# Transposing the FFN's gated values by VectorE blocks and a way through DRAM instead of by TensorE

## The chip, the cores and the metric

The kernel runs on one core of one Trainium2 chip. The core has five engines that work side by side, each through its own list of instructions in order: TensorE (PE, matrix products; PEld is its load of weights), VectorE (DVE), ScalarE (ACT), GpSimd (POOL) and SyncE (SP), which here issues the DMA transfers of the weights. The metric is the device time of one execution in microseconds (us), the median of several.

## The reference

Two layers of a decoder trunk for 256 tokens of width 1024, all in float32. In each layer stand two SwiGLU FFNs, one before and one after the token mixers and the cross attention:

```
D_FF = ((8 * D_MODEL // 3 + 127) // 128) * 128        # 2816

def swiglu(x, w_gate, w_up, w_down):
    return (jax.nn.silu(x @ w_gate) * (x @ w_up)) @ w_down

for l in range(DEPTH):                                # 2
    h = h + 0.5 * swiglu(rms_norm(h, ffn1_norm[l]), ffn1_w_gate[l], ffn1_w_up[l], ffn1_w_down[l])
    ...
    h = h + 0.5 * swiglu(rms_norm(h, ffn2_norm[l]), ffn2_w_gate[l], ffn2_w_up[l], ffn2_w_down[l])
return rms_norm(h, final_norm)
```

So four FFNs are computed. The change touches only what lies between the product of gate and up and the product with `w_down`: that product needs the gated values with the 2816 hidden columns on the partitions, and the gate and up products leave them with the tokens there.

## The kernel before

Every operand of a large product is split into a high and a low part (float32r), and a product is three matmuls: high by high, low by high, high by low. The weights come in **chunks** of 2048 columns by 128 partitions (1 MB). `fetch` loads a chunk into `wr` on SyncE's queue (3 buffers), ScalarE copies it to `wh` in two halves, and VectorE writes the rest to `wl`, also in halves (3 buffers each).

`linear` goes over the chunks and, within a chunk, over the two blocks of 128 tokens. For one chunk and one block it issues 12 matmuls of 128x512 into a PSUM bank `lin`; this is a **half tile**, and `begin` and `tick` around it count the clock `now` by which the other chains of work go on. After the last chunk it calls `evac` for each block.

`ffn` computes the 2816 hidden columns in 11 **groups** of 256. One group is two chunks: 512 columns, 256 of gate and 256 of up, for 1024 input rows. Groups 0 and 1 share a pass, so chunks 0 to 3 belong to both; group g from 2 on uses chunks 2g and 2g+1. Then two passes of six chunks each multiply by `w_down`. `evac` makes `sg` (silu of gate, ScalarE) and `toks` (`sg` times up, VectorE) per token block, and after the second block starts the chain `hidden`. Two half tiles later `hidden` lets PE transpose the four 128x128 blocks into a PSUM bank `ht`, and ScalarE and VectorE split that into `hid`, which the down passes read.

PE works in the order in which the program is written. The order of the other engines' instructions is made by a scheduler when the program is built. Each engine then keeps to its order and waits by semaphores where an operand or a buffer is not there yet.

Of the kernel before, what the change touches and what calls it, by code (L numbers as in the profile page):

```python
# [11 lines left out]
F32 = mybir.dt.float32  # L12
# [7 lines left out]
P = 128  # L20
# [3 lines left out]
NB = S // P  # L24
KD = D // P
DFF = 2816
KF = DFF // P
# [125 lines left out]
def program(tc, a, out, upto="all"):  # L153
    nc = tc.nc
    act, dve, pool, pe = nc.scalar, nc.vector, nc.gpsimd, nc.tensor
    ctx = ExitStack()

    def sb(name, bufs):
        return ctx.enter_context(tc.tile_pool(name=name, bufs=bufs))
# [6 lines left out]
    fp = sb("fp", 2)  # L166
    sp = sb("sp", 4)
    mp = sb("mp", 11)
    lin = ctx.enter_context(tc.tile_pool(name="lin", bufs=4, space=PSUM))
    aux = ctx.enter_context(tc.tile_pool(name="aux", bufs=4, space=PSUM))  # L170
    ctx.enter_context(tc.manual_schedule(engines={mybir.EngineType.PE}))
# [4 lines left out]
    def bank(name):  # L176
        return aux.tile([P, 512], F32, tag="aux", name=name)

    def m4(name, dtype=F32):
        return mp.tile([P, 1024], dtype, tag="m", name=name)  # L180
# [7 lines left out]
    def f2(name, tag="f", bufs=5):  # L188
        return fp.tile([P, 512], F32, tag=tag, name=name, bufs=bufs)
# [9 lines left out]
    ident = cp.tile([P, P], F32, tag="ident", name="ident")  # L199
# [21 lines left out]
    def pcol(l, name, i=0, n=1):  # L221
        o = l * NPC + PO[name][0] + i
        return pcs[:, o:o + n]
# [18 lines left out]
    def advance(c):  # L242
        try:
            c[1] = next(c[0])
            c[2] = now
        except StopIteration:
            chains.remove(c)
# [6 lines left out]
    def start(gen):  # L254
        c = [gen, 0, now]
        chains.append(c)
        advance(c)
        return c

    def begin():  # L260
        nonlocal now
        now += 1

    def tick():
        for c in list(chains):
            if c in chains and ready(c):
                advance(c)

    def finish(c):
        while c in chains:  # L270
            assert isinstance(c[1], int) or all(e in events for e in c[1]), c[1]
            advance(c)
# [12 lines left out]
    def plan():  # L285
# [16 lines left out]
        for l in range(L):  # L302
            yield from ffn(l, "1")
            yield from chunks([win[l, G_QK], win[l, G_RV]], KD, 512)
            yield from chunks([win[l, G_RG]], KD, 512)
            yield from chunks([a["wmisc"][l]], KD, MISC)
            for g in (G_X0, G_X1):
                yield from chunks([win[l, g]], KD, 512, HELD)
            yield from chunks([win[l, G_Z]], KD, 512)
            yield from branch(l, 0)  # L310
            yield a["wmla"][l], 1536, 0
            for g in (G_DQ, G_DK):
                yield from chunks([win[l, g]], KD, 512, HELD)
            yield from chunks([win[l, G_DV]], KD, 512)
            for i in range(1, 4):
                yield from branch(l, i)
            yield from chunks([a["w_out"][l, c] for c in range(2)], KD, 512)
            for n in ("xa_wk", "xa_wq", "xa_wv"):
                for c in range(2):
                    yield from chunks([a[n][l, c]], KD, 512, 0 if n == "xa_wv" else HELD)  # L320
            yield from chunks([a["xa_wo"][l, c] for c in range(2)], KD, 512)
            yield from ffn(l, "2")
# [31 lines left out]
    def weights(n):  # L354
        for _ in range(AHEAD - len(fetched)):
            fetch()
        hi, lo, m = fetched.pop(0)
        assert m == n
        return hi, lo


    def split(hi, lo, src):

        act.activation(hi, src, AF.Copy)
        dve.tensor_tensor(lo, src, hi.bitcast(F32), ALU.subtract)

    def linear(kt, n, xT, evacs):

        ps = [[lin.tile([P, 512], F32, tag="lin", name="lin") for _ in range(NB)] for _ in evacs]
        per = 2048 // n  # L370
        for k0 in range(0, kt, per):
            m = min(per, kt - k0)
            for p_, evac in zip(ps, evacs):
                hi, lo = weights(m * n)
                if now < 4:

                    begin()
                    for k in range(m):
                        for b in range(NB):
                            for part, w in ((0, hi), (1, hi), (0, lo)):  # L380
                                pe.matmul(p_[b][:, :n], lhsT=xT(part, k)[:, b * P:(b + 1) * P],  # L381
                                          rhs=w[:, k * n:(k + 1) * n], start=k == 0 and w is hi and part == 0, stop=False)
                    tick()
                    begin()
                    tick()
                    continue
                for b in range(NB):
                    begin()
                    for part, w in ((0, hi), (1, hi), (0, lo)):
                        for k in range(m):  # L390
                            first = k0 + k == 0 and w is hi and part == 0
                            last = k0 + k == kt - 1 and w is lo
                            pe.matmul(p_[b][:, :n], lhsT=xT(part, k0 + k)[:, b * P:(b + 1) * P],  # L393
                                      rhs=w[:, k * n:(k + 1) * n], start=first, stop=last)
                    if k0 + m == kt:
                        evac(b, p_[b][:, :n])
                    tick()
# [33 lines left out]
    def blk(b):  # L431
        return slice(b * P, (b + 1) * P)
# [91 lines left out]
    def norm(l, name):  # L524
        return Transposed(hh, pcol(l, name, 0, 8), "r" + name)

    def add_to_h(c, factor, nxt, wait=1):
        def evac(b, ps):
            nonlocal paced
            if factor == 1.0:  # L530
                paced = dve.tensor_tensor(h[b][c], ps, h[b][c], ALU.add)  # L531
            else:
                paced = dve.scalar_tensor_tensor(h[b][c], ps, factor, h[b][c], ALU.mult, ALU.add)
            if nxt is not None and b == NB - 1:
                nxt.begin(c, wait)
        return evac

    def ffn(xT, nxt):
        hid = {}

        def hidden(g, toks):
            yield 2
            t4 = m4("hid", F32R).rearrange("p (s f t) -> p s f t", s=2, f=2)
            ps = bank("ht").rearrange("p (f t) -> p f t", f=2)
            for b in range(NB):
                for k in range(2):
                    pe.transpose(ps[:, k, blk(b)], toks[:, b, k * P:(k + 1) * P], ident)  # L547
            split(t4[:, 0], t4[:, 1], ps)
            hid[g] = t4

        def group(g):
            toks = f2("toks", "toks", 3).rearrange("p (b t) -> p b t", b=2)

            def evac(b, ps):
                nonlocal paced
                sg = fp.tile([P, 256], F32, tag="sg", name="sg")
                act.activation(sg, ps[:, :256], AF.Silu, scale=xT.r[:, b:b + 1])  # L557
                paced = dve.scalar_tensor_tensor(toks[:, b], ps[:, 256:], xT.r[:, b:b + 1], sg, ALU.mult, ALU.mult)  # L558
                if b == NB - 1:
                    start(hidden(g, toks))  # L560

            return evac

        linear(KD, 512, xT, [group(0), group(1)])
        for g in range(2, 11):
            linear(KD, 512, xT, [group(g)])
        for c in range(2):
            linear(KF, 512, lambda part, k: hid[k // 2][:, part, k % 2, :], [add_to_h(c, 0.5, nxt, 1 if c else 5)])


    def tables():
# [671 lines left out]
    x = Given(hh, pcol(0, "ffn1", 0, 8), "rffn1")  # L1243
# [13 lines left out]
    for l in range(L):  # L1257
        n = norm(l, "mix")
        ffn(x, n)
        if stages == 1:  # L1260
            break
        x = norm(l, "xa")
        mem, m = mixers(l, n, x)
        if stages == 2:
            break
        n = norm(l, "ffn2")
        cross(l, mem, m, x, n)
        if stages == 3:
            break
        x = norm(l + 1, "ffn1") if l + 1 < L else None  # L1270
        if x is None:
            fn = bias.rearrange("p h k -> p (h k)")[:, :D]
            act.dma_start(fn, a["fnorm"])
        ffn(n, x)
        if stages == 4:
            break
# [17 lines left out]
```

## Time and profile before

| | |
|---|---|
| median of 3 runs | 1585.8 us (1585.21 to 1585.86) |
| the profiled execution | 1585.53 us |
| its span in the trace | 1583.4 us |
| busy share of the span | PE 99%, PEld 85%, VectorE 67%, ScalarE 52%, GpSimd 2% |
| granted TensorE clock, mean | 0.998 |
| moved by DMA | 284.73 MB, 180 GB/s in the mean |

The span goes from the first to the last thing that the profiler saw; some 2.1 us of the execution lie around it. The shares are averages over stages of different kinds. A busy PE need not be one at its peak, since matmuls overlap. The granted clock is a share of TensorE's full 2.4 GHz.

### The profile page before, as it was taken

How to read it: one execution, taken by the hardware profiler on the slowest of the kernel's cores; microseconds unless marked ns; L12 is line 12 of the kernel's file. 1: busy time of each engine (PE TensorE's matmuls, PEld its weight loads, DVE VectorE, ACT ScalarE, POOL GpSimd, SP SyncE). 2: the span in 40 equal slices, each digit the busy share in tenths (PEclk: the TensorE clock that was granted, in tenths of full speed). 3: DMA queues.
4: the chain of work that ended last, by engine and by line, in shares of the span. 5: the costliest groups of instructions: out<-in, count | busy, mean ns of one | idle time of the engine just before them, and what ended most of it. 6: DMA issues, size and time to landing. Idle time of an engine off the chain costs nothing.

```text
span 1583.4 us, 20797 instructions
## 1 busy us (share of the span) xinstructions
PE 1572.2 (99%) x8208; PEld 1345.1 (85%) x8208; DVE 1065.2 (67%) x1704; ACT 830.2 (52%) x1236; POOL 26.0 (2%) x40
## 2 busy tenths in 40 slices
PE   9999999999999999999999999999999999999998
PEld 7888889898888988888888888898988899888886
DVE  5887699997787656554565546697656766565543
ACT  6744446566655545444454444475575555554443
POOL 0000000000000000000000000000000000000000
PEclk9999999999999999999999999999999999999999
DMA  7655544444655444555555556444546554455552
GB/s 291 239 180 179 194 169 160 165 164 144 212 214 177 169 160 163 187 182 182 191 188 188 183 176 209 151 159 157 184 149 237 186 186 164 156 182 176 191 174 74
DMA packets 43153, 284.73 MB, mean 180 GB/s; under 512 B 4784, under 2 KB 5168, under 8 KB 11056
## 3 DMA queue, kind: packets, MB, share of 16 engines
q1 hardware_dynamic: 40464, 276.12, 51.3%
q10 hardware_dynamic: 2592, 7.29, 1.4%
q8 instruction: 64, 1.05, 0.3%
q14 instruction: 33, 0.27, 0.0%
HBM read 282.34 MB, written 1.05 MB: 179 GB/s over the span
## 4 chain that ended last, share of the span: by engine, by line
PE 98%; DMA 1%; ACT 0%; DVE 0%; issue 0%; POOLq 0%; POOL 0%; ACTq 0%
PE lin L393 77%; PE lin L411 11%; PE tr L422 2%; PE ht L547 1%; PE xo L1191 1%; PE lin L381 1%; PE xs L1145 1%; DMA bcs<-bcols 1%; PE up L953 1%; PE my L869 0%; PE ds L1038 0%; PE ms L989 0%; PE pt L680 0%; DMA pcs<-pcols 0%; ACT wh L350 0%
## 5 line engine op out<-in xcount | busy, mean ns | idle before, releaser
L351 DVE TENSOR_TENSOR wl<-wr,wh 128x1024 fp32r<-128x1024 f32 (+3 forms) x536 | 624.7, 1191 | 375.1 <-ACT wh L350 372.7
L350 ACT ACTIVATE wh<-wr 128x1024 fp32r<-128x1024 f32 (+3 forms) x536 | 533.2, 1030 | 493.4 <-PE lin L393 381.7
L393 PE MATMUL lin<-wh,xh 128*128 128x512 f32 (+1 forms) x1200 | 328.5, 395 | 1.1 <-ACT wh L350 0.9
L393 PE MATMUL lin<-wl,xh 128*128 128x512 f32 (+1 forms) x1200 | 320.7, 389 | 0.6 <-DVE wl L351 0.6
L393 PE MATMUL lin<-wh,xl 128*128 128x512 f32 (+1 forms) x1200 | 320.4, 389 | 0.0
L393 PEld LDWEIGHTS lin<-wl,xh 128*128 128x128 f32 x1200 | 225.1, 188 | 48.0 <-DVE wl L351 1.4
L393 PEld LDWEIGHTS lin<-wh,xl 128*128 128x128 f32 x1200 | 225.3, 188 | 47.0
L393 PEld LDWEIGHTS lin<-wh,xh 128*128 128x128 f32 x1200 | 219.2, 188 | 43.7 <-ACT wh L350 2.2
L393 PE MATMUL lin<-wh,hid 128*128 128x512 f32 x704 | 176.0, 390 | 0.0
L393 PEld LDWEIGHTS lin<-wh,hid 128*128 128x128 f32 x704 | 131.6, 188 | 27.1
L393 PE MATMUL lin<-wl,hid 128*128 128x512 f32 x352 | 95.4, 389 | 0.0
L393 PEld LDWEIGHTS lin<-wl,hid 128*128 128x128 f32 x352 | 66.1, 188 | 13.9
L557 ACT ACTIVATE sg<-lin,rffn 128x256 f32<-128x256 f32 x88 | 40.9, 464 | 65.0 <-PE lin L393 63.7
L644 DVE SCALAR_TENSOR_TENSOR bias<-ge,d,bias 128x384 f32<-128x384 f32 x124 | 69.4, 610 | 0.3
L411 PE MATMUL lin<-xh,wh 128*128 128x256 f32 x384 | 62.0, 283 | 0.0
L558 DVE SCALAR_TENSOR_TENSOR toks<-lin,rffn,sg 128x256 f32<-128x256 f32 x88 | 42.3, 480 | 27.7 <-ACT sg L557 27.6
L411 PE MATMUL lin<-xh,wl 128*128 128x256 f32 x384 | 60.5, 279 | 0.0
L411 PE MATMUL lin<-xl,wh 128*128 128x256 f32 x384 | 60.5, 279 | 0.0
L411 PEld LDWEIGHTS lin<-xh,wh 128*128 128x128 f32 x384 | 52.0, 188 | 0.3
L411 PEld LDWEIGHTS lin<-xl,wh 128*128 128x128 f32 x384 | 51.7, 188 | 0.0
L411 PEld LDWEIGHTS lin<-xh,wl 128*128 128x128 f32 x384 | 51.7, 188 | 0.0
L444 ACT ACTIVATE junk<-h 128x512 bf16<-128x512 f32 x36 | 22.4, 623 | 30.6 <-DVE h L531 16.9
(395 smaller groups left out, 1559.4 us busy)
## 6 DMA issues: line engine op xcount, KB each, us to landing
wr<-gu SPq DMA_DIRECT2D x86, 1024.0 KB, 5.1
wr<-win SPq DMA_DIRECT2D x68, 1024.0 KB, 5.1
wr<-dn SPq DMA_DIRECT2D x40, 1024.0 KB, 4.9
wr<-wbr SPq DMA_DIRECT2D x16, 1024.0 KB, 4.9
wr<-w_out SPq DMA_DIRECT2D x8, 1024.0 KB, 5.2
wr<-xa_wk SPq DMA_DIRECT2D x8, 1024.0 KB, 4.9
wr<-xa_wq SPq DMA_DIRECT2D x8, 1024.0 KB, 4.9
wr<-xa_wv SPq DMA_DIRECT2D x8, 1024.0 KB, 5.0
```

The lines of the kernel that those rows point to most:

```text
L350: last = act.activation(hi[:, s], r[:, s], AF.Copy)
L351: dve.tensor_tensor(lo[:, s], r[:, s], hi[:, s].bitcast(F32), ALU.subtract)
L381: pe.matmul(p_[b][:, :n], lhsT=xT(part, k)[:, b * P:(b + 1) * P], rhs=w[:, k * n:(k + 1) * n], start=k == 0 and w is hi and part == 0, sto ...
L393: pe.matmul(p_[b][:, :n], lhsT=xT(part, k0 + k)[:, b * P:(b + 1) * P], rhs=w[:, k * n:(k + 1) * n], start=first, stop=last)
L411: pe.matmul(ps[i][:, j * 256:(j + 1) * 256], lhsT=ws[w][:, o:o + P], rhs=xT(part, k0 + k), start=k0 + k + part + w + j == 0, stop=k0 + k = ...
L422: pe.transpose(ps[:, k * P:(k + 1) * P], src[:, k * P:(k + 1) * P], ident)
L444: act.activation(j[:, :src.free_size()], src, AF.Square, accum_out=out_)
L547: pe.transpose(ps[:, k, blk(b)], toks[:, b, k * P:(k + 1) * P], ident)
L557: act.activation(sg, ps[:, :256], AF.Silu, scale=xT.r[:, b:b + 1])
L558: paced = dve.scalar_tensor_tensor(toks[:, b], ps[:, 256:], xT.r[:, b:b + 1], sg, ALU.mult, ALU.mult)
L644: dve.scalar_tensor_tensor(bias[:, hd], ge, d8[:, hd, i + 1:i + 2], bias[:, hd], ALU.mult, ALU.add)
L953: pe.matmul(ps[:, :n], lhsT=lowT[p_][:, k0 + k, blk(b)], rhs=wm[w][:, o + k * n:o + (k + 1) * n], start=i == 0, stop=i == len(seq) - 1)
```

## The change

In `ffn`, VectorE transposes each token block's `toks` (128x256) in blocks of 32 by 32 into a new tile `turned` right behind `toks`. `hidden` no longer uses PE. Two half tiles later it issues four stores on SyncE's queue, one for each 32 partitions, that write `turned` to a DRAM tile `rows` (each 256 rows of 256 bytes), so that the blocks come to their places; another two half tiles later it issues one load from `rows` into a tile `hidt` (128 partitions, two rows of 1 KB each), also on SyncE's queue; and after another two half tiles ScalarE and VectorE split `hidt` into `hid`, now in two pieces. The load waits for its four stores. The down passes finish a chain `hidden` that is still under way when they need its `hid`. `turned` uses the buffers `gate` (4), `hidt` the buffers `half` (2), both shared with other stages.

```diff
--- before.py
+++ after.py
@@ -166,6 +166,7 @@
     fp = sb("fp", 2)
     sp = sb("sp", 4)
     mp = sb("mp", 11)
+    dp = ctx.enter_context(tc.tile_pool(name="dp", bufs=4, space=bass.MemoryType.DRAM))
     lin = ctx.enter_context(tc.tile_pool(name="lin", bufs=4, space=PSUM))
     aux = ctx.enter_context(tc.tile_pool(name="aux", bufs=4, space=PSUM))
     ctx.enter_context(tc.manual_schedule(engines={mybir.EngineType.PE}))
@@ -536,36 +537,54 @@
         return evac
 
     def ffn(xT, nxt):
-        hid = {}
-
-        def hidden(g, toks):
+        hid, started = {}, {}
+
+        def hidden(g, turned):
+
+            yield 2
+            rows = dp.tile([2 * P, 256], F32, tag="rows", name="rows")
+            w = rows.rearrange("(k j a) (i t) -> i a (k j) t", k=2, j=4, i=4)
+            r = turned.rearrange("p (k t) -> p k t", k=8)
+            for i in range(4):
+                nc.sync.dma_start(w[i], r[i * 32:(i + 1) * 32])
+            yield 2
+            t = f2("hidt", "half", 2)
+            nc.sync.dma_start(t.rearrange("p (k t) -> p k t", k=2), rows.rearrange("(k p) t -> p k t", k=2))
             yield 2
             t4 = m4("hid", F32R).rearrange("p (s f t) -> p s f t", s=2, f=2)
-            ps = bank("ht").rearrange("p (f t) -> p f t", f=2)
-            for b in range(NB):
-                for k in range(2):
-                    pe.transpose(ps[:, k, blk(b)], toks[:, b, k * P:(k + 1) * P], ident)
-            split(t4[:, 0], t4[:, 1], ps)
+            for f in range(2):
+                hi, lo = (x.rearrange("p (c i t) -> p c i t", c=2, i=4) for x in (t4[:, 0, f], t4[:, 1, f]))
+                split(hi, lo, t[:, f * 256:(f + 1) * 256].rearrange("p (i c t) -> p c i t", c=2, i=4))
             hid[g] = t4
 
         def group(g):
             toks = f2("toks", "toks", 3).rearrange("p (b t) -> p b t", b=2)
+
+            turned = f2("turned", "gate", 4)
 
             def evac(b, ps):
                 nonlocal paced
                 sg = fp.tile([P, 256], F32, tag="sg", name="sg")
                 act.activation(sg, ps[:, :256], AF.Silu, scale=xT.r[:, b:b + 1])
                 paced = dve.scalar_tensor_tensor(toks[:, b], ps[:, 256:], xT.r[:, b:b + 1], sg, ALU.mult, ALU.mult)
+                r = turned.rearrange("p (k j c t) -> p c k j t", j=4, k=2, c=2)[:, b]
+                dve.transpose(r, toks[:, b].rearrange("p (k j t) -> p k j t", k=2, j=4))
                 if b == NB - 1:
-                    start(hidden(g, toks))
+                    started[g] = start(hidden(g, turned))
 
             return evac
 
         linear(KD, 512, xT, [group(0), group(1)])
         for g in range(2, 11):
             linear(KD, 512, xT, [group(g)])
+
+        def hT(part, k):
+            if k // 2 not in hid:
+                finish(started[k // 2])
+            return hid[k // 2][:, part, k % 2, :]
+
         for c in range(2):
-            linear(KF, 512, lambda part, k: hid[k // 2][:, part, k % 2, :], [add_to_h(c, 0.5, nxt, 1 if c else 5)])
+            linear(KF, 512, hT, [add_to_h(c, 0.5, nxt, 1 if c else 5)])
 
 
     def tables():
```

The scheduler's order changes with it. The rows below are from the second FFN (the one behind the cross attention of the first layer), around groups 3 to 5. The number behind a name is that of the tile.

ScalarE before: `sg_5862` and `sg_5877` are the two token blocks of group 3, `sg_5943` and `sg_5958` those of group 4; `wh_5965` and `wh_6005` are the chunks of group 5, `wh_6046` and `wh_6086` those of group 6.

```order
L557 ACTIVATE sg_5862<-lin_5800,rffn2_5599 128x256
L350 ACTIVATE wh_5965<-wr_5964 128x1024
L557 ACTIVATE sg_5877<-lin_5801,rffn2_5599 128x256
L350 ACTIVATE wh_5965<-wr_5964 128x1024
L350 ACTIVATE wh_6005<-wr_6004 128x1024 x2
L364 ACTIVATE hid_5915<-ht_5916 128x512
L557 ACTIVATE sg_5943<-lin_5881,rffn2_5599 128x256
L350 ACTIVATE wh_6046<-wr_6045 128x1024
L557 ACTIVATE sg_5958<-lin_5882,rffn2_5599 128x256
L350 ACTIVATE wh_6046<-wr_6045 128x1024
L350 ACTIVATE wh_6086<-wr_6085 128x1024 x2
L364 ACTIVATE hid_5996<-ht_5997 128x512
```

Both chunks of group 5 stand ahead of the first `sg` of group 4, and half of group 6's first chunk ahead of its second.

ScalarE after the change: `sg_5972` is the second token block of group 3, `sg_6044` and `sg_6060` are those of group 4, and `sg_6132` the first of group 5. `wh_6025` is the second chunk of group 4, `wh_6071` and `wh_6113` are the chunks of group 5, and `wh_6159` the first of group 6.

```order
L568 ACTIVATE sg_5972<-lin_5893,rffn2_5680 128x256
L351 ACTIVATE wh_6025<-wr_6024 128x1024
L365 ACTIVATE hid_6014<-hidt_5976 128x256 x2
L351 ACTIVATE wh_6025<-wr_6024 128x1024
L568 ACTIVATE sg_6044<-lin_5980,rffn2_5680 128x256
L568 ACTIVATE sg_6060<-lin_5981,rffn2_5680 128x256
L351 ACTIVATE wh_6071<-wr_6070 128x1024 x2
L365 ACTIVATE hid_6102<-hidt_6064 128x256 x2
L351 ACTIVATE wh_6113<-wr_6112 128x1024 x2
L365 ACTIVATE hid_6190<-hidt_6152 128x256 x2
L351 ACTIVATE wh_6159<-wr_6158 128x1024
L568 ACTIVATE sg_6132<-lin_6068,rffn2_5680 128x256
```

Both chunks of group 5 now stand behind the second `sg` of group 4, and a piece of `hid` stands between them.

SyncE before: from the second chunk of group 4 (`wr_5923`) on, `wr_5964` and `wr_6004` are the chunks of group 5.

```order
L343 DMA wr_5923<-gu2 128x2048
L343 DMA wr_5964<-gu2 128x2048
L343 DMA wr_6004<-gu2 128x2048
L343 DMA wr_6045<-gu2 128x2048
L343 DMA wr_6085<-gu2 128x2048
L343 DMA wr_6126<-gu2 128x2048
```

SyncE after the change: `rows_5931` is stored from group 2's gated values, `rows_6019` from group 3's and `rows_6107` from group 4's. `wr_6024` is the second chunk of group 4, `wr_6070` and `wr_6112` are those of group 5, `wr_6158` and `wr_6200` those of group 6. Only weights stood here before.

```order
L344 DMA wr_6024<-gu2 128x2048
L552 DMA hidt_5976<-rows_5931 128x2x256
L549 DMA rows_6019<-turned_5891 32x8x64 x4
L344 DMA wr_6070<-gu2 128x2048
L552 DMA hidt_6064<-rows_6019 128x2x256
L549 DMA rows_6107<-turned_5979 32x8x64 x4
L344 DMA wr_6112<-gu2 128x2048
L552 DMA hidt_6152<-rows_6107 128x2x256
L344 DMA wr_6158<-gu2 128x2048
L344 DMA wr_6200<-gu2 128x2048
L344 DMA wr_6246<-gu2 128x2048
```

The load of group 5's first chunk moved behind the stores of group 3, and that of its second chunk behind the stores of group 4; four loads follow without a store between them.

## Rows read from the trace of the kernel before

**Rows 1.** The page, parts 1 and 4: busy time by engine; chain by engine.

```profile
PE 1572.2 (99%) x8208; PEld 1345.1 (85%) x8208; DVE 1065.2 (67%) x1704; ACT 830.2 (52%) x1236; POOL 26.0 (2%) x40
...
PE 98%; DMA 1%; ACT 0%; DVE 0%; issue 0%; POOLq 0%; POOL 0%; ACTq 0%
```

**Rows 2.** The chain in order of time, 60 to 95 us: start, us, what.

```profile
60.82 10.93 PE lin L393 x48
71.75 0.44 PE ht L547 x4
72.19 10.93 PE lin L393 x48
```

**Rows 3.** Who waited for whom: engine and line, us in total, times, longest.

```profile
ACT wh L350 <- PE lin L393: 381.7, 170, 4.3
```

**Rows 4.** Groups of instructions by line, shapes apart (columns as on the page).

```profile
L350 ACT ACTIVATE wh<-wr 128x1024 fp32r<-128x1024 f32 x500 | 509.0, 1053 | 462.8 <-PE lin L393 354.8 <-issue 77.3 <-PE lin L411 22.4
...
L644 DVE SCALAR_TENSOR_TENSOR bias<-ge,d,bias 128x384 f32<-128x384 f32 x124 | 69.4, 610 | 0.3
...
L547 PE MATMUL ht<-ident,toks 128*128 128x128 f32 x176 | 26.3, 271 | 0.0
...
L1155 DVE TENSOR_SCALAR xpr<-xpr,xrs 128x256 f32<-128x256 f32 x16 | 4.9, 351 | 0.3
```

**Rows 5.** Timeline of the fourth FFN, 1440.5 to 1445.5: start, duration.

```profile
1440.58 2.01 ACT L350 ACTIVATE wh<-wr 128x1024 fp32r<-128x1024 f32 x2 [3.07 <-PE lin L393]
...
1443.57 1.08 PE L393 MATMUL lin<-wl,xh 128*128 128x512 f32 x4
...
1444.49 1.07 PE L393 MATMUL lin<-wh,xh 128*128 128x512 f32 x4
1444.69 0.47 ACT L557 ACTIVATE sg<-lin,rffn 128x256 f32<-128x256 f32 x1 [1.62 <-PE lin L393]
...
1445.20 0.48 DVE L558 SCALAR_TENSOR_TENSOR toks<-lin,rffn,sg 128x256 f32<-128x256 f32 x1 [0.57 <-ACT sg L557]
```

**Rows 6.** Timeline of the first FFN, 23 to 25.5 us.

```profile
23.80 1.99 ACT L350 ACTIVATE wh<-wr 128x1024 fp32r<-128x1024 f32 x2
...
24.89 0.73 PE L393 MATMUL lin<-wh,xh 128*128 128x512 f32 x2 [0.93 <-ACT wh L350]
```

**Rows 7.** SyncE's DMA issues by source line: ns min/median/max; us to landing.

```profile
L343 SPq DMA_DIRECT2D wr<-gu x86: 327/328/430, 7.2 to 1484.5; - x86
...
DMA to landing us min/median/max: 3.5/5.0/10.1
...
L1252 SPq DMA_DIRECT2D h<-x x4: 328/436/504, 7.7 to 10.4; - x4
...
L1233 SPq DMA_DIRECT2D out<-fin x2: 344/346/348, 1578.1 to 1579.6; - x2
...
DMA to landing us min/median/max: 2.1/2.3/2.5
```

**Rows 8.** The page, part 3: DMA queues (packets, MB, share of 16 engines).

```profile
q1 hardware_dynamic: 40464, 276.12, 51.3%
q10 hardware_dynamic: 2592, 7.29, 1.4%
```

**Rows 9.** Windows at the program's end: PEclk is the column after POOL.

```profile
1575.50:1576.00 0.50, 0.40 (x2) 0.00 (x0) 0.07 (x1) 0.50 (x2) 0.00 (x0) 1.00 0.00 0
1577.50:1578.00 0.50, 0.00 (x0) 0.00 (x0) 0.50 (x1) 0.50 (x1) 0.00 (x0) 1.00 0.00 0
1578.00:1578.50 0.50, 0.00 (x0) 0.00 (x0) 0.17 (x2) 0.07 (x1) 0.25 (x1) 0.74 0.00 0
1578.50:1579.00 0.50, 0.00 (x0) 0.00 (x0) 0.16 (x1) 0.16 (x1) 0.30 (x1) 0.50 0.07 25
```

**Rows 10.** Window of the third FFN: busy us (instructions), PEclk, DMA share, GB/s.

```profile
815.00:963.00 148.00, 148.00 (x679) 122.55 (x678) 78.99 (x87) 67.45 (x88) 0.00 (x0) 1.00 0.56 187
```

## The prediction

> **What bounds the kernel now.** I read the page first, for the engine without gaps: TensorE (PE) is busy 99% of the span and holds 98% of the chain that ended last [rows 1]. Time is therefore won by taking PE work out and lost by leaving PE with nothing to do. The profiled execution took 1585.53 us (span 1583.4, 2.1 around it), against a median of 1585.8; I sum from the first.
>
> Then the chain in order of time, for one step of the gate-and-up part: 48 `lin` matmuls take 10.93 us, four `ht` transposes stand behind them for 0.44 us, and the next step begins 11.37 us after the last [rows 2]. So a matmul is worth 10.93 / 48 = 0.228 us, a half tile (12) 2.73 us, a weights chunk (24) 5.46 us.
>
> Then the list of waits, for how far the weights are ahead: ScalarE's split of a chunk waited for PE 170 times, 381.7 us in all [rows 3]. It waits to get a `wh` buffer back, so finished chunks stand ready in front of PE. This lead is what the change spends.
>
> **What it removes.** 4 FFNs x 11 groups = 44 times four transposes. The group of lines gives 26.3 us for the 176 [rows 4], but matmuls overlap; on the chain they are worth 0.44 us each time: 44 x 0.44 = **19.4 us won**.
>
> **What it adds off the path.** VectorE gets 88 block transposes of 128x256. No row shows one; below it is a plain one-operand pass of that shape, 0.35 us, above it the 0.61 us of a 128x384 pass with two tensors [rows 4]. I take 0.48 us, a two-operand pass of the same shape [rows 5]. ScalarE's split of `hid` becomes two of half the size. In an FFN window of 148 us VectorE is busy 79 and ScalarE 67 [rows 10], so as busy time this costs nothing; it counts only where it stands between PE and its next weights. The Trainium skill, "VectorE: DVE Perf Modes", section "The three transpose paths", gives 311 ns for a 128x128 bf16 transpose on VectorE. Twice that, as an estimate for twice the elements, would put some 0.14 us into each of the nine places below, 1.3 us in the sum; no run here shows it yet.
>
> The DMA engines get 1024 rows of 256 bytes and 256 of 1 KB per group. Two queues give the price of a packet: 51.3% of 16 x 1583.4 us for 40464 packets and 276.12 MB, and 1.4% for 2592 packets and 7.29 MB [rows 8]. Solved for a price per packet and one per byte, that is about 8 ns and 46 ps, so 20 ns for 256 bytes: 64 packets on each engine, 1.3 us a group. The other bound is the 137 ns that the second queue's packets take on average: 8.8 us a group. I take the first, because the solved price says that these packets' time is nearly all bytes. The DMA share in an FFN is 0.56 [rows 10]; 1.3 us and 0.9 us for the reads, of 11 us, leave room.
>
> **What it puts on the path.** This I read from the order excerpts. Before, a chunk's load has no other SyncE work ahead of it, and its split stands on ScalarE up to two chunks ahead of the group that uses it. After, the loads stand in line behind the `rows` stores of earlier groups. In the second FFN's group 4, ScalarE's order is both `sg`, and only then the split of group 5's first chunk (`wh_6071`); SyncE's order is the four stores of group 4 (`rows_6107`) and only then the load of group 5's second chunk (`wr_6112`). PE comes to the end of group 4 with no chunk ready. I call that a dry crossing. Its price, from t = 0 where group 4's last matmul ends:
>
> 1. `sg` starts 0.04 after the modelled end of the last matmul (1444.65 to 1444.69) and takes 0.47; the next matmul began 0.16 before that end [rows 5]. The first half of `wh` takes 1.05 [rows 4], and the matmul starts 0.04 behind it [rows 6]. PE starts at 0.04 + 0.47 + 0.04 + 1.05 + 0.04 = 1.64, so it has lost 1.8. It uses this half up in two matmuls (0.46) and waits for the other, which ends at 0.55 + 2.01 = 2.56 [rows 5]: 0.5 more. **2.3 us**. The chunk is used up at -0.16 + 2.3 + 5.46 = 7.6.
> 2. The second chunk: `toks` ends at 1.03 and the block transpose at about 1.55. Then come four stores. An issue of a 128x512 tile on SyncE took 0.33 to 0.50, median 0.44 [rows 7]; with 0.05 between them the load is issued at 3.5. A load lands 5.0 after its issue in the median [rows 7]: 8.5. A half split gives 9.6, the matmul 9.65, 2.05 late, and its second half 0.5 more. **2.55 us**.
>
> Together 4.85 us. What is queued behind: the read `hidt` waits for its stores to land (2.3 us for the only stores that the trace has [rows 7]), at about 5.8, and the next load stands behind it. It lands near 12 (1 MB keeps the 16 engines for 3.0 us by the price per byte in [rows 8], and the load before it holds them until 8.5), and PE wants that chunk at 15, so nothing more is late; from there SyncE's order has four loads in a row, and the lead is back until the next crossing.
>
> I went through the order of all four FFNs for such places: the first has three (from group 2 to 3, 6 to 7, and 10 to the down projection), the others two each (4 to 5, 8 to 9): nine. Between them one chunk is always split before its group begins. 9 x 4.85 = **43.7 us lost**.
>
> Sum: 1585.5 - 19.4 + 43.7 = **1609.8 us**.
>
> Bounds of one crossing: with 0.33 per issue, 0.35 for the transpose and everything else as above it is 4.35, which gives 1605.2. With twice the median issue, for twice as many rows in a store (0.88), and 0.61 for the transpose it is 6.8, which gives 1627. The mixers' order on ScalarE is unchanged, so I put nothing there.
>
> **The rivals.**
>
> *The crossings are longer.* Two mechanisms, one result. (a) A 256-byte store costs far more than its bytes. At 137 ns a packet the stores keep each engine for 8.8 us from about 1.9 on, to 10.7, and the load behind them in the same queue, with its own 3.0, lands near 14 instead of 8.5: a crossing of 10.4, 9 x 10.4 = 93.6, 1660 us. Against it is the solved price of 8 ns; for it, that no row times packets so small. The Trainium skill, "DMA: Bandwidth & Descriptors", section "Specifications", says that a transfer under 512 B is not at line rate, since the DMA engine then reads, modifies and writes; by that rule the stores here, of 256 B, would be of the slow kind, and no row of the kernel before can confirm it. (b) PE's clock falls in the gaps. At the end of the program the granted clock was still 1.00 up to 1578.0, went to 0.74 in the next half us and to 0.50 after it (1.2 GHz, not 2.4); the last matmuls began in 1575.5 to 1576.0 [rows 9]. So it fell some 2.3 us after the last work. A crossing's gaps are 1.8 and 2.05, just short of that. If it fell each time and cost a chunk at half speed (5.46), 9 x 5.46 = 49 more: 1659.
>
> *The crossings cost only their first part.* If the second chunk lands in time, nine times 2.3 is 20.7, against 19.4 won: 1586.8, no change. This needs the load to land by 6.5, with its issue at 3.5: 3.0 after issue. The shortest of all loads took 3.5 [rows 7].
>
> *Faster.* The mechanism would be the lead: a crossing is dry only if PE has used up what was split ahead, and the order says in which sequence an engine works, not how far it is in time. If only the three crossings of the first FFN were dry, where VectorE also has other work between, 3 x 4.85 = 14.6 is lost and the kernel takes 1580.7. The point that decides is 19.4 / 4.85 = 4.0 dry crossings. Against it: in all nine places the split stands behind a `sg` of the group that has just ended, on an engine that works in order, so it cannot have been done before.
>
> **How the numbers follow.** Forecast as summed, 1600 to 1627: 0.56. Longer crossings, 1627 to 1660: 0.30. First part alone, 1582.6 to 1600: 0.09, of which 0.06 is within 0.2% (3.2 us either side, about what a measurement of this kernel can tell from no change). Faster: 0.05. The range for 8 in 10 is 1601 to 1648: it leaves out the two small cases and the far end of the long crossings, 2 in 10 in all. Slower by over 0.2%: 0.89.
>
> **What would show it.** The `ht` rows are gone and PE's busy time is lower by about 26 us, while the span is longer. In each FFN, PE has gaps at the crossings named, and nowhere else: first some 1.8 us that end with ScalarE's `wh`, a short one of 0.5, and 5.5 us later one of about 2 that ends with `wh` again, where ScalarE itself had waited for the DMA `wr`. SyncE shows waits of the stores for VectorE's block transpose, and the load behind them issued about 3.5 us after the group's end. Crossings of 4.85 confirm the sum; a late load with a short issue would point to the packets, matmuls of twice the length to the clock. The prediction is wrong if PE's gaps are spread over all 44 groups (the DMA system would be the bound), or if there are fewer than nine.

## The result and the profile after

| | |
|---|---|
| median of 4 runs after | 1622.8 us (1622.63 to 1625.15) |
| before, beside them | 1585.83 us (1585.21 to 1585.93) |
| ratio | 1.0237, 95% interval 1.022 to 1.0255 |
| span of the profiled execution | 1620.8 us (before 1583.4) |

The change costs 37 us. The time is 13 us above the 1609.8 that was forecast, and inside the range of 1601 to 1648.

The page of the kernel after, parts 1 and 4, as [rows 1] of before:

```profile
PE 1573.5 (97%) x8032; PEld 1332.5 (82%) x8032; DVE 1103.7 (68%) x1836; ACT 835.8 (52%) x1280; POOL 26.1 (2%) x40
...
PE 91%; DMA 3%; ACT 2%; DVE 2%; SPq 1%; issue 1%; POOLq 0%; POOL 0%; DVEq 0%; ACTq 0%
```

PE has 176 instructions fewer, and yet 1.3 us more busy time; its share of the chain falls from 98% to 91%. DMA's share has grown from 1% to 3%, and ScalarE, VectorE and SyncE's issues have entered the chain, though none of them is busier than 68%.

The waits after (the first two rows are ScalarE's, the third PE's; us in total, times, longest), as [rows 3]:

```profile
ACT wh L351 <- PE lin L394: 224.5, 101, 7.0
...
ACT wh L351 <- DMA wr<-gu: 68.7, 26, 6.9
...
PE lin L394 <- ACT wh L351: 34.2, 36, 4.3
```

And the waits of SyncE's queue:

```profile
SPq L549 <- DVE turned L571: 183.4, 37, 8.1
```

Before, ScalarE's splits waited 170 times for PE to give a buffer back. Now it is 101 times; in 26 cases ScalarE waits for the load instead, and PE for ScalarE. SyncE stands for 183.4 us in front of stores whose data are not yet made, with weights behind them in its list.

The timeline of PE at the first crossing of the second FFN, group 4 to 5 (start, duration, what, idle before and its releaser):

```profile
679.68 1.07 PE L394 MATMUL lin<-wl,xh 128*128 128x512 f32 x4
682.26 0.73 PE L394 MATMUL lin<-wh,xh 128*128 128x512 f32 x2 [1.51 <-ACT wh L351]
683.21 0.73 PE L394 MATMUL lin<-wh,xh 128*128 128x512 f32 x2 [0.21 <-ACT wh L351]
...
690.56 0.73 PE L394 MATMUL lin<-wh,xh 128*128 128x512 f32 x2 [2.07 <-ACT wh L351]
691.51 0.74 PE L394 MATMUL lin<-wh,xh 128*128 128x512 f32 x2 [0.22 <-ACT wh L351]
```

And the chain of the same place, in order of time (start, us, what):

```profile
680.79 0.48 ACT sg L568
...
681.30 0.49 DVE toks L569
...
681.81 0.46 DVE turned L571
...
682.28 0.31 SPq L549
...
682.65 0.44 SPq L549
...
683.13 0.52 SPq L549
...
683.70 0.47 SPq L549
...
684.22 5.21 DMA wr<-gu
...
689.45 2.01 ACT wh L351 x2
```

The first listing shows both parts of a dry crossing, the second the way of its second part: `sg`, `toks`, block transpose, four stores, and only then the load, issued 3.5 us after the group's end. The load needs 5.21 us, where the median before was 5.0, so it is not a slow one [rows 7]. The crossing's price: the last matmul of group 4 ended at 682.26 - 1.51 = 680.75; undisturbed, the next would have begun 0.16 before that, at 680.59. The second chunk began at 690.56, and 690.56 - 680.59 - 5.46 (the first chunk's matmuls) = 4.5; with 0.5 for its second half it is 5.0 us. Gaps of this form, in two parts, stand at the nine places named and at no other group's end; only the first FFN has further ones, which end with VectorE's `wl`.

How late each stretch is can be read from the transposes of the norms (`tr` x8 on the chain) behind each FFN. The last column is a run told of below, in which the same work is done and no crossing is dry.

| | before | after | path issued by GpSimd | lost by the order |
|---|---|---|---|---|
| first FFN ends | 178.52 | 197.97 | 173.93 | 24.0 |
| second begins | 602.33 | 621.78 | 597.74 | 0 |
| second ends | 775.46 | 801.68 | 765.51 | 12.1 |
| third ends | 962.18 | 993.09 | 946.88 | 10.0 |
| fourth begins | 1386.45 | 1417.36 | 1371.16 | 0 |
| end of the span | 1583.4 | 1620.8 | 1563.2 | 11.4 |

The loss lies in the four FFNs alone, 57.6 us in all, against a gain of 1583.4 - 1563.2 = 20.2.

### The profile page after: what moved, and what is told of

Read it like the earlier page. It is cut to its first block, busy times and chain, and to the rows that moved or that the text cites. A ratio compares the mean times of both kernels' runs of the same rounds, so it can differ in the third digit from the quotient of the medians.

```text
span 1620.8 us, 20973 instructions
## 1 busy us (share of the span) xinstructions
PE 1573.5 (97%) x8032; PEld 1332.5 (82%) x8032; DVE 1103.7 (68%) x1836; ACT 835.8 (52%) x1280; POOL 26.1 (2%) x40
## 4 chain that ended last, share of the span: by engine, by line
PE 91%; DMA 3%; ACT 2%; DVE 2%; SPq 1%; issue 1%; POOLq 0%; POOL 0%; DVEq 0%; ACTq 0%
PE lin L394 72%; PE lin L412 11%; DMA wr<-gu 3%; PE tr L423 2%; ACT wh L351 1%; SPq L549 1%; PE xo L1210 1%; PE xs L1164 1%; PE lin L382 1%; PE up L972 1%; DVE bias L663 0%; PE my L888 0%; PE ds L1057 0%; DVE wl L352 0%; ACT sg L568 0%
## 5 line engine op out<-in xcount | busy, mean ns | idle before, releaser
L571 DVE STREAM_TRANSPOSE turned<-toks 128x256 f32<-128x256 f32 x88 | 39.0, 443 | 1.9
```

What stands on the lines that cost most here:

```text
L571: dve.transpose(r, toks[:, b].rearrange("p (k j t) -> p k j t", k=2, j=4))
```

## The experiments

The theory: what is lost is PE's waiting at the dry crossings, made by the *order* on ScalarE and SyncE; the work added costs nothing by itself. The main rivals: the path's transfers cost the time, wherever they are issued (256-byte packets, DMA traffic), or VectorE's and ScalarE's added work does; and the clock.

**The transposition left out.** The kernel before, in which `hid` is split straight from `toks` (in SBUF); this leaves out the transposition, and nothing else of the products.

```diff
-            ps = bank("ht").rearrange("p (f t) -> p f t", f=2)
-            for b in range(NB):
-                for k in range(2):
-                    pe.transpose(ps[:, k, blk(b)], toks[:, b, k * P:(k + 1) * P], ident)
-            split(t4[:, 0], t4[:, 1], ps)
+            split(t4[:, 0], t4[:, 1], toks)
```

> The kernel before, without the four TensorE transposes of each group and with nothing in their place: hid is split straight from toks, so the transposition is left out of the computation. Both theories use this as the size of what is won. If the 0.44 us per group on the chain is the worth of the transposes, 44 x 0.44 = 19.4 us go: 1566.4 us. If they lay in a shadow, 1585.8 us.

Measured: 1563.37 us, ratio 0.986 (0.9845 to 0.9875), span 1561.3. So leaving the transposition out wins 22.1 us of span (1583.4 - 1561.3), 3 us more than was expected. The second FFN takes 167.77 instead of 173.13: 5.36 / 11 = 0.49 us a group, where the chain's 0.44 was taken. The first FFN gains 6.1.

**The path in GpSimd's queue.** The change, with stores and read issued by GpSimd, whose list has little else in it.

```diff
-                nc.sync.dma_start(w[i], r[i * 32:(i + 1) * 32])
+                nc.gpsimd.dma_start(w[i], r[i * 32:(i + 1) * 32])
...
-            nc.sync.dma_start(t.rearrange(...), rows.rearrange(...))
+            nc.gpsimd.dma_start(t.rearrange(...), rows.rearrange(...))
```

> The change, with its stores and its reads issued by GpSimd instead of SyncE. By the order of this kernel no split of a group's first chunk stands behind the sg of the group before it, so no crossing is dry. Theory of the dry crossings: all of the loss goes and the 19.4 us won are left, 1566 to 1570 us. Rival (the 256-byte stores, the added DMA traffic and VectorE's transposes cost the time themselves): the work is all still there, so it stays above 1600 us.

Measured: 1564.3 us (1563.66 to 1564.97), ratio 0.9866 (0.9852 to 0.9881). It beats the kernel before and the change, is 1.7 us below the range given (more is won than the 19.4 that the range took), and is 0.9 us from the run with no transposition at all. Its page, parts 3, 4 and 6:

```profile
q1 hardware_dynamic: 40464, 276.12, 52.2%
q0 software_dynamic: 9152, 23.08, 4.4%
...
PE 97%; DMA 1%; ACT 1%; issue 0%; DVE 0%; POOL 0%; SPq 0%; POOLq 0%; ACTq 0%
...
rows<-turned POOLq DMA_DIRECT2D x176, 64.0 KB, 4.4
hidt<-rows POOLq DMA_DIRECT2D x44, 256.0 KB, 4.2
```

The stores land *later* here (4.4 us after issue, 1.9 on SyncE's queue), and it does no harm: `hid` is wanted only by the down passes. VectorE's transposes and the 23 MB are all there. What the change loses, it loses by where the issues stand. This run alone changes two things, the queue and the order; the next one keeps the queue.

**Weights fetched three chunks ahead, path on SyncE.** `AHEAD` is the number of chunks for which `linear` asks in advance.

```diff
-AHEAD = 1
+AHEAD = 3
```

> The change, with the stores and reads on SyncE as they are, but the program asks for weights three chunks ahead (AHEAD = 3 instead of 1). By its order no crossing is dry. Theory of the dry crossings: 1566 to 1572 us. Rival one (traffic and VectorE work): above 1600 us. Rival two (it is enough for a loss that stores wait in the same queue as the weights, whatever the order of the splits): 1585 to 1600 us.

Measured: 1575.23 us, ratio 0.9934 (0.9917 to 0.9951). From the start of the second FFN to its end it takes 776.44 - 608.67 = 167.77 us, the very time of the run with GpSimd's queue and of the run without transposition: there, on SyncE's queue and with 256-byte stores, a path whose issues do not stand ahead of a wanted load costs nothing. The run is 3 us above the range given; what it lacks to the GpSimd run lies in the first FFN, which ends at 184.85 (173.93 with GpSimd's queue). PE's timeline there:

```profile
34.91 2.05 PE L394 MATMUL lin<-wh,xh 128*128 128x512 f32 x4 [5.90 <-DVE toks L569]
```

At the opening the splits of the chunks fetched in advance stand ahead of the first `toks` on VectorE (the chain there goes through `wh`, a norm's `junk` and `wl` for some 10 us before `toks` begins at 34.37), and PE waits for `toks` to read its PSUM bank.

**The control: the kernel before with `AHEAD = 3`.**

> The kernel before with AHEAD = 3: a control for the run of the change with AHEAD = 3, whose first FFN ended 10.9 us later than with the path in GpSimd's queue. If fetching ahead alone delays the first FFN (its inputs' transfers stand behind more weights at the opening): 1585.5 + 10 = 1595 to 1597, all of it before the first mixer. If it was the path through DRAM together with the deeper fetch: 1585.5, within 0.2%.

Measured: 1590.52 us, ratio 1.0033 (1.002 to 1.0046). This is neither of the two times expected. The first FFN ends 5.0 later than before, the rest takes the same time. Its PE has a gap at the same place, which ends with the same `toks`:

```profile
33.94 1.12 PE L547 MATMUL ht<-ident,toks 128*128 128x128 f32 x4 [5.23 <-DVE toks L558]
```

So the opening pays for the depth with or without the path, but only 5.0 of the 10.9; I had said 10. The other 5.9 belong to the path and depth together. In the run of the change with depth three, VectorE's `wl` is late three times more (gaps of 0.39, 0.39 and 1.46, each with 0.40 for its second half, 3.4 us in all), and behind the last of them the granted clock falls to 0.50 from 147 to 151 us, which takes another 1.7; this is read from the trace and was not tried by itself.

**The change in the second FFN alone.** The others keep PE's transposes (`ffn_pe` is `ffn` of before).

```diff
-        ffn(x, n)
+        ffn_pe(x, n)
...
-        ffn(n, x)
+        (ffn if l == 0 else ffn_pe)(n, x)
```

> The change is made in the second FFN alone; the other three keep TensorE's transposes. Its order has two crossings at which the next chunk's split and the second chunk's load stand behind the path's work (after groups 4 and 8 of that FFN), so if the loss is made crossing by crossing it is 1585.5 - 4.84 (44 transposes' quarter: 11 of 0.44 us) + 2 x 5.1 = 1590.9, and 1592.3 if TensorE's clock falls behind the gaps as in the run of the change, where this FFN ended 6.77 us later. Rival: the loss comes from the four FFNs' traffic together, or from the first FFN's opening, and one FFN alone is quicker by its transposes: 1580.7.

Measured: 1592.6 us, ratio 1.0049 (1.0036 to 1.0061). The FFN takes 179.96 us, in the change itself 179.90: this FFN pays for its own crossings, with nothing carried over from the first. The rival with 1580.7 falls. PE's gaps (the second crossing is like it):

```profile
662.91 0.73 PE L394 MATMUL lin<-wh,xh 128*128 128x512 f32 x2 [1.51 <-ACT wh L351]
...
671.29 0.73 PE L394 MATMUL lin<-wh,xh 128*128 128x512 f32 x2 [2.16 <-ACT wh L351]
```

**Two chunks ahead.** This takes the two parts apart: the loads are early, and the split of the next group's first chunk still stands behind the second `sg`, at twelve places.

```diff
-AHEAD = 1
+AHEAD = 2
```

> The change with AHEAD = 2, weights fetched two chunks ahead. In its order the second chunk's load never stands behind the stores, but the split of the next group's first chunk still stands behind the second sg at twelve places (after groups 4, 7 and 10 of each FFN). So it takes the two parts of a crossing apart. If part one costs its 2.3 us alone: 1564 (the same path with no crossing) + 12 x 2.3 = 1591.6, and up to 1602 if fetching ahead also costs the first FFN what it cost with AHEAD = 3 (10.9 us). Rival: part one costs nothing by itself, since what is lost is the load's way (5.2 us from issue to landing) and the split only fills the time before it: 1564 to 1575.

Measured: 1607.54 us, ratio 1.0145 (1.013 to 1.0161). PE's timeline in the second FFN, the first two of its three gaps:

```profile
675.61 0.73 PE L394 MATMUL lin<-wh,xh 128*128 128x512 f32 x2 [1.51 <-ACT wh L351]
676.56 0.74 PE L394 MATMUL lin<-wh,xh 128*128 128x512 f32 x2 [0.22 <-ACT wh L351]
710.55 0.73 PE L394 MATMUL lin<-wh,xh 128*128 128x512 f32 x2 [1.51 <-ACT wh L351]
711.50 0.72 PE L394 MATMUL lin<-wh,xh 128*128 128x512 f32 x2 [0.21 <-ACT wh L351]
```

No gap follows 7.6 us later. The FFN takes 789.84 - 615.13 = 174.71, that is 6.94 more than 167.77: 2.31 for each of three. Part one costs by itself what was summed for it, 2.3. The total is above the 1602 that I gave as the far end. In the profiled execution, the fastest of the four (1604.28), the first FFN ends 17.4 later than in the GpSimd run: three crossings of 2.3, and 10.5 for its opening, VectorE's lateness and falls of the clock.

**The bias table later.** In the first FFN VectorE also builds a bias table for the second mixer. Here it begins after half tile 72, so that it no longer meets the crossings.

```diff
-            yield 3
+            yield 2
...
-            while 60 <= now < 72:
+            while now < 72:
```

> The change, with the bias table's threshold work on VectorE moved out of the first FFN into the mixers (it begins at half tile 72, every two half tiles). The nine dry crossings stand in the order as before. If the excess of the first FFN's second and third crossing comes from this VectorE work between the block transposes and the splits, about 5 us go, 1617 to 1619 us, and the first FFN is shorter by as much in its trace. If that excess has another cause, 1622 to 1624 us.

Measured: 1638.91 us, ratio 1.0334 (1.0317 to 1.0351). As a version it is a miss: the table comes too late for the differential attention, and PE stands there for 13 us, then works on at the lower clock (0.50) for some 6 us more.

```profile
450.23 0.74 PE L699 MATMUL pt<-ident,dsb 128*128 128x128 f32 x2 [13.04 <-DVE dsb L1069]
```

But the first FFN, for which it was made, ends at 192.72, 5.25 earlier than in the change, and its gaps for `wl` are gone. So where VectorE's table work stands accounts for 5.25 of the 24.0 us that this FFN loses.

**GpSimd's queue and two chunks ahead.**

> The path in GpSimd's queue and AHEAD = 2. With the path off SyncE no crossing is left, and the kernel without any transposition took 1563.4, so nothing below some 1562 is to be had: 1562 to 1565 if the depth of the fetch costs nothing, 1567 to 1575 if it costs the first FFN a part of what AHEAD = 3 did.

Measured: 1565.1 us (1564.03 to 1565.89), ratio 0.9873 (0.9859 to 0.9886). Nothing more is to be had by depth; the first FFN ends 0.9 later than with `AHEAD = 1`, the rest is equal.

## Why the prediction was right, and where its sum was short

**The win.** 19.4 was said. The whole transposition is worth 22.1 us of span, 20.2 with the path in its place. The chain's 0.44 was a little too small; a group gains 0.49.

**Costs off the path.** Said: nothing, as busy time. The GpSimd run shows it: the work added costs 0.9 us by the medians and 1.9 by the profiled spans (1563.2 - 1561.3). Of these, 1.5 lie in the first FFN (173.93 against 172.43), where PE stands once for 1.56 us; the second FFN takes 167.77 with the path and without. The block transpose took less than the 0.48 taken for it (line group of the kernel after: busy, mean ns, idle):

```profile
L571 DVE STREAM_TRANSPOSE turned<-toks 128x256 f32<-128x256 f32 x88 | 39.0, 443 | 1.9
```

The Trainium skill, "VectorE: DVE Perf Modes", section "The three transpose paths", led to an estimate of 0.62 us; the measured 0.443 decides against doubling its figure.

**The packets.** Said: 8 ns and 46 ps per byte, not 137 ns. The page after, parts 3 and 6:

```profile
q1 hardware_dynamic: 100304, 299.20, 55.9%
...
rows<-turned SPq DMA_DIRECT2D x176, 64.0 KB, 1.9
```

Against [rows 8] that is 59840 packets and 23.08 MB more, and 0.559 x 16 x 1620.8 - 0.513 x 16 x 1583.4 = 1500 us of engine time. At 46 ps the bytes take 1062, which leaves 438 us, about 7 ns a packet; at 137 ns it would be 8200 us. The rival with slow stores falls. The Trainium skill, "DMA: Bandwidth & Descriptors", section "Specifications", gives 512 B as the least transfer for line rate, which speaks for that rival. The packets added here took 1.4 times the time of their bytes (1500 against 1062), and the price per packet that [rows 8] gave for the queues before is enough for that.

**The crossings.** Said: nine, at named places, 2.3 + 2.55 = 4.85 each. All nine are there and no others. Part one alone measured 2.31; part two was not run alone and is the difference. For the six in the second to fourth FFN, worked out as above from their gaps, a crossing is 4.8 to 5.2, together 30.0 against 29.1. The mechanism and its size hold there. (By its own terms, 0.33 per issue and 0.35 for the transpose, the lower bound is 4.28 and not 4.35; nothing hangs on it.)

**The signs.** One of them failed: PE's busy time was to be lower by about 26 us, and it is 1.3 higher. In the GpSimd run it is 20.9 lower (1551.3). The crossings add busy time to PE: at the lower clock a matmul lasts longer, and in front of a gap the trace counts 0.73 us for two matmuls that take some 0.46 in an unbroken row. How much each adds was not worked out.

**What failed** is the sum of 43.7 us lost: it is 57.6, which is 13.9 more. Two steps of it failed.

The first is the clock. The prediction took the gaps for "just short" of the 2.3 us after which it had fallen at the program's end, and put the clock at nothing in the sum. It fell behind shorter gaps. Windows of 1 us behind the second crossing of the second FFN (PE, PEld, DVE, ACT, POOL busy, then PEclk):

```profile
740.00:741.00 1.00, 0.79 (x4) 0.51 (x4) 1.00 (x2) 0.96 (x3) 0.00 (x0) 0.97 1.02 426
741.00:742.00 1.00, 1.00 (x4) 0.81 (x3) 1.00 (x2) 0.00 (x0) 0.00 (x0) 0.50 0.97 410
742.00:743.00 1.00, 1.00 (x4) 0.81 (x3) 0.46 (x2) 0.83 (x1) 0.00 (x0) 0.50 1.05 442
743.00:744.00 1.00, 1.00 (x4) 0.71 (x4) 0.74 (x1) 0.23 (x1) 0.00 (x0) 0.50 1.01 328
744.00:745.00 1.00, 1.00 (x5) 0.83 (x4) 0.49 (x1) 0.42 (x2) 0.00 (x0) 0.83 0.97 393
```

PE had stood still for 1.51 and, 7 us later, for 2.22 us; the granted clock went from full (2.4 GHz) to 0.50 (1.2 GHz), where four matmuls take 1.91 instead of 1.07. The missing shares add up to 0.03 + 3 x 0.50 + 0.17 = 1.70 us. The clock fell so once in each of the second to fourth FFN and three times in the first, where the first fall lasted twice as long. This is the mechanism of the rival (b) at a third of its price (1.7, not 5.46). Not each fall is paid either: in the third FFN it fell between the two parts of a crossing, PE was slower with the first chunk, and the wait for the second was 0.37, where it was 2.07 at the first crossing of the second FFN: 1.70 less.

```profile
878.80 1.91 PE L394 MATMUL lin<-wl,xh 128*128 128x512 f32 x4
...
883.98 0.73 PE L394 MATMUL lin<-wh,xh 128*128 128x512 f32 x2 [0.37 <-ACT wh L351]
```

So the falls in the second and fourth FFN (3.4 us) and the last in the first (1.7) are paid: 5.1 of the 13.9 us. With that the six crossings come to 30.0 + 3.4 = 33.4, against 12.1 + 10.0 + 11.4 = 33.5 in the table.

The second is the first FFN, for which the same price was taken three times (14.6), and which lost 24.0. ScalarE's timeline at its first crossing:

```profile
38.69 1.28 ACT L568 ACT_TABLE_LOAD   x1 [0.35 <-PE lin L394]
39.98 0.47 ACT L568 ACTIVATE sg<-lin,rffn 128x256 f32<-128x256 f32 x1
...
40.68 1.28 ACT L639 ACT_TABLE_LOAD   x1
...
42.09 0.71 ACT L365 ACTIVATE hid<-hidt 128x256 fp32r<-128x256 f32 x2
42.81 1.28 ACT L568 ACT_TABLE_LOAD   x1
44.10 0.47 ACT L568 ACTIVATE sg<-lin,rffn 128x256 f32<-128x256 f32 x1
44.48 1.99 ACT L351 ACTIVATE wh<-wr 128x1024 fp32r<-128x1024 f32 x2
```

Between its two `sg` ScalarE loads tables for other work and splits a `hid`, so PE's gap is 4.25 instead of 1.51, and the crossing, worked out as above, 8.6. Before, the split stood ahead of all this (ScalarE's timeline there, then three chunks in a row):

```profile
35.11 5.78 ACT L350 ACTIVATE wh<-wr 128x1024 fp32r<-128x1024 f32 x6
```

The second crossing is 6.2 and the third 5.3, and after the third PE waits for VectorE, whose list there is, with PE's wait below it:

```profile
153.62 4.32 DVE L663 SCALAR_TENSOR_TENSOR bias<-ge,d,bias 128x384 f32<-128x384 f32 x8
157.85 2.36 DVE L352 TENSOR_TENSOR wl<-wr,wh 128x1024 fp32r<-128x1024 f32 x2
...
159.13 0.73 PE L394 MATMUL lin<-wl,hid 128*128 128x512 f32 x2 [2.31 <-DVE wl L352]
```

Eight bias steps, 4.32 us together, stand ahead of a `wl` that PE wants (a gap of 2.31, and 0.40 for the second half: 2.7). The three crossings, this wait and one paid fall of the clock make 8.6 + 6.2 + 5.3 + 2.7 + 1.7 = 24.5 against the 24.0 lost; smaller waits, here and in the GpSimd run, were not balanced. The run with the later table shows VectorE's part, 5.25 us: its second and third crossing are 4.9 and 5.0, and the wait of 2.7 is gone. The clock has no share in this, since there too one fall is paid, behind the second crossing (the change, then the run with the later table):

```profile
162.00:163.00 1.00, 1.00 (x4) 0.81 (x3) 1.00 (x2) 0.00 (x0) 0.00 (x0) 0.50 0.78 319
...
106.00:107.00 1.00, 1.00 (x3) 0.79 (x3) 0.53 (x2) 0.00 (x0) 0.00 (x0) 0.50 1.01 426
```

That the table loads make the first crossing long is read from the trace and was not tried by itself.

That the time still fell into the band of 1600 to 1627, to which the forecast gave its largest chance, is in part luck. The upper half of that band stood for longer issues and a longer block transpose (0.88 and 0.61 us). Both came out near or below the values of the sum, 0.45 (median) and 0.44, and what filled the band was put at nothing:

```profile
L549 SPq DMA_DIRECT2D rows<-turned x176: 302/452/1876, 26.7 to 1556.5; - x176
```

**The rivals.** "First part alone" falls with the second gaps; "faster, only three dry" falls with the gaps at all nine places and with the run of the second FFN alone.

## What to carry to other kernels

Cost an off-path addition by where its instructions and DMA issues stand in each in-order list, not by its busy time: here work that costs one or two us in an idle queue cost 57.6 us more ahead of weights in a busy one. Count the places at which a wanted load or split stands behind something that cannot be ready yet, price one step by step, and look at each engine's other work there, since one place is not like another. In this kernel, issues that wait for data belonged on an engine with nothing urgent behind them.

## What the runs showed of the hardware

- In SyncE's queue the 59840 packets added, most of them rows of 256 bytes, cost about 7 ns each beside their bytes (an estimate from the queues' shares). The same 23.08 MB issued by GpSimd went in 9152 packets, with 0.58 us of GpSimd for a store, and a store landed 4.4 us after its issue instead of 1.9.
- The granted clock fell to 0.50 behind gaps of 1.5 to 2.3 us, in some crossings and not in others with like gaps (the first of the fourth FFN, 1.51 and 2.21, stayed at 1.00). What decides it is open.
- In the third FFN a fall of the clock ahead of a wait cost nothing: the 1.70 us that PE lost were missing in that wait (0.37 instead of 2.07).
